# RMSNorm on one core: uneven tiles, a third tile loaded in 29 and 2 rows, and a first store that waits for the 29

## The chip, the core and the metric

The kernel runs on one core of one Trainium2 chip. The metric is the device time of one execution in microseconds (us), as the median of repeated runs. A separate execution, taken with the hardware profiler, gives the profile and the trace. In a profile PE is the matrix engine, DVE the vector engine, ACT the scalar engine, POOL the GpSimd engine and SP the engine that issues all DMAs of this kernel.

## The reference

```python
batch, seq, dim = 16, 1024, 512
x = np.random.randn(batch, seq, dim).astype(np.float32)      # 33.55 MB
gamma = np.ones(dim, dtype=np.float32)

def reference(x, gamma):
    eps = 1e-5
    rms = np.sqrt(np.mean(x ** 2, axis=-1, keepdims=True) + eps)
    return (x / rms * gamma).astype(np.float32)
```

There are 16384 rows of 512 numbers. Each is divided by the root of its mean square and multiplied by gamma. All of x is read once and all of the output is written once, 67.1 MB in total.

## The kernel before

**Tiles.** The 16384 rows are cut into 4 tiles of 4096 rows. In a tile each of the 128 partitions holds R = 32 consecutive rows of 2 KB, so that a partition's part of a tile is one stretch of 64 KB in memory. Below, "a row" means one row in each of the 128 partitions, which is 256 KB. The whole kernel loads 128 such rows and stores 128.

**Buffers.** Three buffers (`slot0` to `slot2`) of 32 rows hold tiles 0, 1 and 2; tile 3 goes into `slot0` again, after tile 0 has been stored from it (`slot_of = [0, 1, 2, 0]`). All work is done in place in these buffers.

**DMA order.** Every load (helper `load`, line 45) and every store (helper `store`, line 49) is issued by SP, in program order, on one queue. A DMA instruction that has to wait for something holds back all later ones on SP. The order is: tile 0 in 1, 15 and 16 rows (gamma's 2 KB after the first two), tile 1 in 16 and 16, tile 2 in 16 and 16; then two stores of 16 rows for tile 0; then two loads of 16 rows for tile 3 into the same buffer, each waiting until the store of those rows has landed; then one store of 32 rows for tile 1, one for tile 2, and two of 16 rows for tile 3. The function `transfers` places those after the first five loads.

**Compute.** The tiles are worked through in 8 groups of 16 rows, written out in the list `groups` as (tile, first row, rows, pieces, POOL's share). For a group, `square_sums` squares pieces of several rows on ACT (L95) into a scratch buffer and adds them up on DVE (L96); `inverse_rms` makes the factor of each row (L101 on ACT, L102 on DVE). Then POOL multiplies its share of rows by the factor and by gamma (L108, L109); ACT multiplies the other rows by the factor, row by row (L117), and DVE multiplies these by gamma (L121). The squares of the next group are interleaved with the scaling of this one.

**Scratch.** The squares go alternately into a PSUM buffer of 7 rows and an SBUF buffer of 5 rows. The two groups of tile 0 have pieces of 7 and 9 rows, and the piece of 9 uses the last rows of `slot2` as scratch, before tile 2 is loaded there:

```python
        if m == 9:
            sq = slots[2][:, 23:32, :]
```

So the load of rows 16 to 32 of tile 2 has to wait until DVE has added up the second such piece; the load of its rows 0 to 16 does not.

Of the kernel before, what the change touches and what calls it, by code (L numbers as in the profile page):

```python
# [8 lines left out]
@with_exitstack  # L9
def kernel(  # L10
    ctx: ExitStack,
    tc: tile.TileContext,
    x: bass.AP,
    gamma: bass.AP,
    out: bass.AP,
):
    nc = tc.nc
    P = nc.NUM_PARTITIONS
    eps = 1e-5
    fp32 = mybir.dt.float32  # L20
    AF = mybir.ActivationFunctionType
    OP = mybir.AluOpType

    xf = x.flatten_outer_dims()
    of = out.flatten_outer_dims()
    N, D = xf.shape
    R = 32
    assert N == 4 * P * R

    xv = xf.rearrange("(t p r) d -> t p r d", p=P, r=R)  # L30
    ov = of.rearrange("(t p r) d -> t p r d", p=P, r=R)

    ctx.enter_context(tc.manual_schedule())
    nc.scalar.addr_align(128, offset=0, max_nops=0)

    const = ctx.enter_context(tc.tile_pool(name="const", bufs=1))
    stats = ctx.enter_context(tc.tile_pool(name="stats", bufs=9))
    psum = ctx.enter_context(tc.tile_pool(name="psum", bufs=1, space=bass.MemoryType.PSUM))

    slots = [const.tile([P, R, D], fp32, name=f"slot{i}") for i in range(3)]  # L40

    before_scale = []

    def load(t, slot, r0, r1):
        dma = nc.sync.dma_start(out=slots[slot][:, r0:r1], in_=xv[t][:, r0:r1])  # L45
        before_scale.append((slot, r0, r1, dma))

    def store(t, slot, r0, r1):
        dma = nc.sync.dma_start(out=ov[t][:, r0:r1], in_=slots[slot][:, r0:r1])
        before_scale.append((slot, r0, r1, dma))  # L50

    gamma_row = const.tile([1, D], fp32)
    pieces = (0, D)

    load(0, 0, 0, 1)
    load(0, 0, 1, 16)
    for c0, c1 in zip(pieces, pieces[1:]):
        nc.sync.dma_start(out=gamma_row[:, c0:c1], in_=gamma.unsqueeze(0)[:, c0:c1])
    load(0, 0, 16, 32)
    load(1, 1, 0, 16)  # L60
    load(1, 1, 16, 32)

    ones_col = const.tile([1, P], fp32)
    nc.gpsimd.memset(ones_col, 1.0)  # L64
    gamma_psum = psum.tile([P, 1, D], fp32, name="gamma_psum")
    nc.tensor.matmul(gamma_psum[:, 0], ones_col, gamma_row, start=True, stop=True)  # L66
    gamma_b = const.tile([P, 1, D], fp32)

    eps_t = const.tile([P, 1], fp32)
    nc.gpsimd.memset(eps_t, eps)  # L70
    table = const.tile([P, 1], fp32)
    nc.scalar.activation(out=table, in_=eps_t, func=AF.Sqrt)  # L72

    groups = [
        (0, 0, 16, (7, 9), 6),
        (0, 16, 16, (7, 9), 7),
        (1, 0, 16, (7, 5, 4), 7),
        (1, 16, 16, (7, 5, 4), 7),  # L80
        (2, 0, 16, (7, 5, 4), 7),
        (2, 16, 16, (7, 5, 4), 7),
        (3, 0, 16, (7, 5, 4), 7),
        (3, 16, 16, (7, 5, 4), 3),
    ]
    slot_of = [0, 1, 2, 0]

    def square_sums(ss, t, g, r, m, k):
        if m == 9:
            sq = slots[2][:, 23:32, :]  # L90
        else:
            home, name, most = ((psum, "sq_psum", 7), (const, "sq_sbuf", 5))[k % 2]
            sq = home.tile([P, most, D], fp32, name=name)
        rows = slots[slot_of[t]][:, g + r : g + r + m, :]
        nc.scalar.activation(out=sq[:, :m], in_=rows, func=AF.Square)  # L95
        nc.vector.tensor_reduce(  # L96
            out=ss[:, r : r + m, 0], in_=sq[:, :m], axis=mybir.AxisListType.X, op=OP.add
        )

    def inverse_rms(ss, n):  # L100
        nc.scalar.activation(out=ss[:, :n, 0], in_=ss[:, :n, 0], func=AF.Sqrt, bias=eps_t, scale=1.0 / D)  # L101
        nc.vector.reciprocal(out=ss[:, :n, 0], in_=ss[:, :n, 0])  # L102
        return ss

    def scale_by_pool(rstd, t, g, n, share):
        part = slots[slot_of[t]][:, g + n - share : g + n, :]
        by_row = rstd[:, n - share : n].to_broadcast([P, share, D])
        nc.gpsimd.tensor_tensor(out=part, in0=part, in1=by_row, op=OP.mult)  # L108
        last = nc.gpsimd.tensor_tensor(  # L109
            out=part, in0=part, in1=gamma_b.to_broadcast([P, share, D]), op=OP.mult  # L110
        )
        before_scale.append((slot_of[t], g + n - share, g + n, last))

    def scale(rstd, t, g, r0, r1):
        x = slots[slot_of[t]]
        for r in range(r0, r1):
            nc.scalar.activation(out=x[:, g + r, :], in_=x[:, g + r, :], func=AF.Copy, scale=rstd[:, r])  # L117

    def times_gamma(t, g, r0, r1):
        part = slots[slot_of[t]][:, g + r0 : g + r1, :]  # L120
        scaled = nc.vector.tensor_tensor(  # L121
            out=part, in0=part, in1=gamma_psum.to_broadcast([P, r1 - r0, D]), op=OP.mult
        )
        for slot, b0, b1, earlier in before_scale:
            if slot == slot_of[t] and b0 < g + r1 and g + r0 < b1:
                tc.declare_no_dep(scaled.ins, earlier.ins, reason="ScalarE waited for it before it scaled these rows")

    def transfers(t, g):
        if (t, g) == (0, 0):
            load(2, 2, 0, 16)  # L130
            load(2, 2, 16, 32)
        elif (t, g) == (0, 16):
            store(0, 0, 0, 16)
            store(0, 0, 16, 32)
            load(3, 0, 0, 16)
            load(3, 0, 16, 32)
        elif (t, g) == (1, 16):
            store(1, 1, 0, 32)
        elif (t, g) == (2, 16):
            store(2, 2, 0, 32)  # L140
        elif (t, g) == (3, 0):
            store(3, 0, 0, 16)
        elif (t, g) == (3, 16):
            store(3, 0, 16, 32)

    def pieces_of(group):
        t, g, n, pieces, share = group
        ss = stats.tile([P, 16, 1], fp32, name="ss")
        r = 0
        todo = []  # L150
        for k, m in enumerate(pieces):
            todo.append((ss, t, g, r, m, k))
            r += m
        return ss, todo

    ss, todo = pieces_of(groups[0])
    for piece in todo:
        square_sums(*piece)
    rstd = inverse_rms(ss, groups[0][2])
    nc.scalar.copy(out=gamma_b[:, 0], in_=gamma_psum[:, 0])  # L160
    for k, group in enumerate(groups):
        t, g, n, pieces, share = group
        mine = n - share
        half = (mine + 1) // 2
        ahead = groups[k + 1 :][:1]
        ss, todo = pieces_of(ahead[0]) if ahead else (None, [])
        scale_by_pool(rstd, t, g, n, share)
        for piece in todo[:2]:
            square_sums(*piece)
        scale(rstd, t, g, 0, half)  # L170
        for piece in todo[2:]:
            square_sums(*piece)
        scale(rstd, t, g, half, mine)
        times_gamma(t, g, 0, mine)
        transfers(t, g)
        for nxt in ahead:
            rstd = inverse_rms(ss, nxt[2])
# [30 lines left out]
```

## Time and profile before

| what | value |
|---|---|
| median of 3 runs | 161.75 us (161.73 to 161.88) |
| profiled execution: its own time | 161.72 us |
| profiled execution: span from the first to the last instruction | 159.9 us |
| bytes moved by DMA | 67.12 MB, 420 GB/s over the span |
| DVE, ACT, POOL busy | 112.8, 109.1, 102.1 us |
| share of the 16 DMA engines' time in data packets | 98.1% |

The profile's times count from the start of the span. An issue row gives the time on SP and the median time from issue to landing, that is to the semaphore which says that the data is there. "DMA share" in a window is the time of the packets that begin in it, so it can exceed 1 in a short window.

### The profile page before, as it was taken

To read this page: it belongs to the slowest core of one execution; us is meant where nothing else is said; L and a number is where in the kernel's file an instruction comes from. 1 tells how busy PE (TensorE), PEld (TensorE's weight loads), DVE (VectorE), ACT (ScalarE), POOL (GpSimd) and SP (SyncE) were. 2 spreads that over 40 slices of the span, in tenths; PEclk is the share of its full clock that TensorE was granted. 3 is DMA by queue.
4 is the path that set the end of the run, shared out by engine and by line. 5 is a ranking of instruction groups with operands and counts; after the bars stand their busy time and mean duration, and the time that the engine had idled before them with its cause. 6 is when DMAs were issued, how large, how long until landed. Compare 5 with 4: busy or idle time off the path is not lost.

```text
span 159.9 us, 258 instructions
## 1 busy us (share of the span) xinstructions
PE 2.0 (1%) x2; PEld 0.5 (0%) x2; DVE 112.8 (71%) x38; ACT 109.1 (68%) x110; POOL 102.1 (64%) x22
## 2 busy tenths in 40 slices
PE   0005000000000000000000000000000000000000
PEld 0001000000000000000000000000000000000000
DVE  0000993797999999999999999999999702950000
ACT  3007906999998899899989989999994297000000
POOL 1000005994079999999999999999999997000000
DMA  5989999999999997999999999997997998999995
GB/s 191 492 369 468 451 393 434 484 393 418 484 410 393 483 426 311 483 393 402 508 402 393 492 426 393 524 475 311 524 459 328 524 426 361 393 459 459 393 426 229
DMA packets 2163, 67.12 MB, mean 420 GB/s; under 512 B 241, under 2 KB 241, under 8 KB 370
## 3 DMA queue, kind: packets, MB, share of 16 engines
q1 hardware_dynamic: 2162, 67.11, 98.1%
q14 instruction: 1, 0.01, 0.0%
HBM read 33.56 MB, written 33.55 MB: 420 GB/s over the span
## 4 chain that ended last, share of the span: by engine, by line
DVE 62%; ACT 18%; DMA 7%; ACTq 0%; SPq 0%; issue 0%
DVE ss L96 36%; DVE slot L121 26%; ACT slot L117 9%; DMA slot<-in_x_dram 7%; ACT slot L95 5%; ACT sq_psum L95 4%; DVE ss L102 1%; ACTq L203 0%; ACT gamma_b L160 0%; SPq L45 0%; ACT ss L101 0%; ACTq L95 0%
## 5 line engine op out<-in xcount | busy, mean ns | idle before, releaser
L108 POOL TENSOR_TENSOR slot<-slot,ss 128x3584 f32<-128x3584 f32 (+2 forms) x8 | 45.0, 5625 | 31.8 <-DVE ss L102 31.8
L96 DVE TENSOR_REDUCE ss<-sq_psum 128x7 f32<-128x3584 f32 (+1 forms) x14 | 44.5, 3176 | 19.5 <-ACT sq_psum L95 19.5
L109 POOL TENSOR_TENSOR slot<-slot,gamma_b 128x3584 f32<-128x3584 f32 (+2 forms) x8 | 56.9, 7112 | 0.6
L117 ACT ACTIVATE slot<-slot,ss 128x512 f32<-128x512 f32 x77 | 48.5, 707 | 4.9 <-DVE ss L102 4.9
L121 DVE TENSOR_TENSOR slot<-slot,gamma_psum 128x4608 f32<-128x4608 f32 (+2 forms) x8 | 42.3, 5282 | 9.3 <-ACT slot L117 9.3
L95 ACT ACTIVATE sq_psum<-slot 128x3584 f32<-128x3584 f32 (+1 forms) x14 | 36.5, 2604 | 11.4 <-DMA slot<-in_x_dram 10.4
L96 DVE TENSOR_REDUCE ss<-sq_sbuf 128x5 f32<-128x2560 f32 x6 | 16.8, 2806 | 0.0
L95 ACT ACTIVATE sq_sbuf<-slot 128x2560 f32<-128x2560 f32 x6 | 13.9, 2320 | 0.0
L96 DVE TENSOR_REDUCE ss<-slot 128x9 f32<-128x4608 f32 x2 | 9.9, 4953 | 0.1
L101 ACT ACTIVATE ss<-ss,eps_t 128x16 f32<-128x16 f32 x8 | 2.4, 306 | 8.4 <-DVE ss L96 8.4
L95 ACT ACTIVATE slot<-slot 128x4608 f32<-128x4608 f32 x2 | 8.1, 4028 | 0.0
L102 DVE RECIPROCAL ss<-ss 128x16 f32<-128x16 f32 x8 | 2.0, 249 | 0.4 <-ACT ss L101 0.4
L66 PE MATMUL gamma_psum<-gamma_row,ones_col 1*128 1x512 f32 x2 | 2.0, 1120 | 12.8 <-DMA gamma_row<-in_gamma_dram 12.8
L72 ACT ACT_TABLE_LOAD x1 | 1.3, 1283 | 1.1 <-PEq L192 1.1
L160 ACT COPY gamma_b<-gamma_psum 128x512 f32<-128x512 f32 x1 | 0.6, 566 | 0.0
L66 PEld LDWEIGHTS gamma_psum<-gamma_row,ones_col 1*128 1x128 f32 x2 | 0.5, 304 | 12.8 <-issue 12.8
L64 POOL MEMSET ones_col<- 1x128 f32 x1 | 0.2, 194 | 0.3 <-POOLq L192 0.3
L192 POOL MEMSET const-float32-0.0<- 128x1 f32 x1 | 0.1, 98 | 0.2 <-issue 0.2
L72 ACT ACTIVATE table<-eps_t 128x1 f32<-128x1 f32 x1 | 0.2, 203 | 0.0
L192 POOL MEMSET const-bfloat16-1.0<- 128x1 bf16 x1 | 0.1, 101 | 0.0
L192 POOL MEMSET const-uint8-127<- 128x1 uint8 x1 | 0.1, 101 | 0.0
L192 POOL MEMSET const-float32-1.0<- 128x1 f32 x1 | 0.1, 98 | 0.0
(1 smaller groups left out, 0.1 us busy)
## 6 DMA issues: line engine op xcount, KB each, us to landing
slot<-in_x_dram SPq DMA_DIRECT2D x7, 4096.0 KB, 27.1
out_dram<-slot SPq DMA_DIRECT2D x4, 4096.0 KB, 21.8
slot<-in_x_dram SPq DMA_DIRECT2D x1, 3840.0 KB, 11.8
slot<-in_x_dram SPq DMA_DIRECT2D x1, 256.0 KB, 3.1
out_dram<-slot SPq DMA_DIRECT2D x2, 29.2
gamma_row<-in_gamma_dram SPq DMA_DIRECT2D x1, 2.0 KB
```

Of the source, the lines that this page charges most:

```text
L66: nc.tensor.matmul(gamma_psum[:, 0], ones_col, gamma_row, start=True, stop=True)
L72: nc.scalar.activation(out=table, in_=eps_t, func=AF.Sqrt)
L95: nc.scalar.activation(out=sq[:, :m], in_=rows, func=AF.Square)
L96: nc.vector.tensor_reduce(out=ss[:, r : r + m, 0], in_=sq[:, :m], axis=mybir.AxisListType.X, op=OP.add)
L101: nc.scalar.activation(out=ss[:, :n, 0], in_=ss[:, :n, 0], func=AF.Sqrt, bias=eps_t, scale=1.0 / D)
L102: nc.vector.reciprocal(out=ss[:, :n, 0], in_=ss[:, :n, 0])
L108: nc.gpsimd.tensor_tensor(out=part, in0=part, in1=by_row, op=OP.mult)
L109: last = nc.gpsimd.tensor_tensor(out=part, in0=part, in1=gamma_b.to_broadcast([P, share, D]), op=OP.mult)
L117: nc.scalar.activation(out=x[:, g + r, :], in_=x[:, g + r, :], func=AF.Copy, scale=rstd[:, r])
L121: scaled = nc.vector.tensor_tensor(out=part, in0=part, in1=gamma_psum.to_broadcast([P, r1 - r0, D]), op=OP.mult)
L160: nc.scalar.copy(out=gamma_b[:, 0], in_=gamma_psum[:, 0])
L192: nc = _bacc.Bacc("TRN2", target_bir_lowering=False, num_devices=1)
```

## The change

The tiles become uneven: 33, 31, 31 and 33 rows per partition. The three buffers have 33, 31 and 31 rows. The second group of each tile has 17, 15, 15 and 17 rows, and its last piece of squares changes by one row. The scratch piece in `slot2` covers rows 21 to 31, of which a piece of 9 uses the first 9 and the new piece of 10 uses all.

Tile 2 is loaded as one DMA of 29 rows and one of 2 rows. The load of 29 rows covers scratch rows, so it waits for DVE, too. The first store (rows 0 to 16 of tile 0) gets an added wait: SP issues it only when the load of the 29 rows has landed.

```diff
-    R = 32
-    xv = xf.rearrange("(t p r) d -> t p r d", p=P, r=R)
-    ov = of.rearrange("(t p r) d -> t p r d", p=P, r=R)
+    rows_of = (33, 31, 31, 33)
+    def by_tile(flat):
+        views, start = [], 0
+        for rows in rows_of:
+            part = flat[start : start + P * rows]
+            views.append(part.rearrange("(p r) d -> p r d", p=P, r=rows))
+            start += P * rows
+        return views
...
-    def store(t, slot, r0, r1):
+    def store(t, slot, r0, r1, behind=None):
         dma = nc.sync.dma_start(out=ov[t][:, r0:r1], in_=slots[slot][:, r0:r1])
+        if behind is not None:
+            tc.add_manual_dep(
+                dma.ins,
+                behind.ins.name,
+                mybir.DependencyInfo(mybir.DependencyClass.Sync, mybir.DependencyReason.DATA),
+                reason="the store is issued when this load has landed",
+            )
...
-        (0, 16, 16, (7, 9), 7),
+        (0, 16, 17, (7, 10), 7),
         (1, 0, 16, (7, 5, 4), 7),
-        (1, 16, 16, (7, 5, 4), 7),
+        (1, 16, 15, (7, 5, 3), 7),
         (2, 0, 16, (7, 5, 4), 7),
-        (2, 16, 16, (7, 5, 4), 7),
+        (2, 16, 15, (7, 5, 3), 7),
         (3, 0, 16, (7, 5, 4), 7),
-        (3, 16, 16, (7, 5, 4), 3),
+        (3, 16, 17, (7, 5, 5), 3),
...
-        if m == 9:
-            sq = slots[2][:, 23:32, :]
+        if m >= 9:
+            sq = slots[2][:, 21:31, :]
...
         if (t, g) == (0, 0):
-            load(2, 2, 0, 16)
-            load(2, 2, 16, 32)
+            gate.append(load(2, 2, 0, 29))
+            load(2, 2, 29, 31)
         elif (t, g) == (0, 16):
-            store(0, 0, 0, 16)
-            store(0, 0, 16, 32)
+            store(0, 0, 0, 16, behind=gate[0])
+            store(0, 0, 16, 33)
             load(3, 0, 0, 16)
-            load(3, 0, 16, 32)
+            load(3, 0, 16, 33)
```

## The prediction

> **What bounds the kernel now.** I read the page's slices first, then the queues.
>
> ```profile
> span 159.9 us, 258 instructions
> ...
> DMA  5989999999999997999999999997997998999995
> GB/s 191 492 369 468 451 393 434 484 393 418 484 410 393 483 426 311 483 393 402 508 402 393 492 426 393 524 475 311 524 459 328 524 426 361 393 459 459 393 426 229
> ...
> q1 hardware_dynamic: 2162, 67.11, 98.1%
> ```
>
> The DMA engines work from the first slice to the last, and their packets fill 98.1% of the span. No compute engine passes 71%. So only DMA time that is idle or stretched can be won, 1.9% of 159.9, about 3 us, start and end included.
>
> Next, the DMA view in narrow windows, each around one issue on SP: bytes and time from issue to landing (loads issued at 2.02 and 38.01, stores at 44.71, 58.95, 86.93, 114.93 and 142.22).
>
> ```profile
> slot<-in_x_dram SPq DMA_DIRECT2D x1, 4096.0 KB, 20.7
> ...
> slot<-in_x_dram SPq DMA_DIRECT2D x1, 4096.0 KB, 24.2
> ...
> out_dram<-slot SPq DMA_DIRECT2D x1, 4096.0 KB, 27.2
> ...
> out_dram<-slot SPq DMA_DIRECT2D x1, 4096.0 KB, 23.0
> ...
> out_dram<-slot SPq DMA_DIRECT2D x1, 33.5
> ...
> out_dram<-slot SPq DMA_DIRECT2D x1, 24.9
> ...
> out_dram<-slot SPq DMA_DIRECT2D x1, 4096.0 KB, 16.9
> ```
>
> Issue plus time gives landings; with the other issues' rows and the longest load (3.40 + 48.4) they are: 16 rows at 13.0 us, 32 at 22.7, 48 at 32.4, 64 at 42.1, 80 at 51.8, 96 at 62.2; stores at 71.9 and 81.95; loads until 101.1; stores at 120.4, 139.8, 149.5 and 159.1. The step is 9.7 us per 16 rows (0.606 per row) nearly everywhere. 51.8 to 62.2 is 10.4: the changeover from loads to the first store costs 0.7 us more than any load step. The second such changeover (101.1 to 120.4 for 32 rows) shows nothing beyond 19.4.
>
> The trace's single packets say the same from nearer. A 32 KB packet takes 1.21 us on each of the 16 DMA engines. Before the first store, the last load packet takes 1.69 to 2.04 us, and on five engines the one before it 0.25 to 0.41 more than normal. On the engine that is last here, the last load packet takes 2.04 (0.83 over) and its first store packet begins at 61.88. Before the second changeover packets are stretched by 0.28 at most, and in the first 9 us by some tenths. Otherwise the packets follow each other without gaps.
>
> **What waits.** The views of DVE and SP around the scratch and around the first stores:
>
> ```profile
> 28.97 4.03 ACT L95 ACTIVATE slot<-slot 128x4608 f32<-128x4608 f32 x1
> ...
> 33.03 4.95 DVE L96 TENSOR_REDUCE ss<-slot 128x9 f32<-128x4608 f32 x1
> 38.01 0.33 SPq L45 DMA_DIRECT2D slot<-in_x_dram  x1
> ...
> 44.71 0.35 SPq L49 DMA_DIRECT2D out_dram<-slot  x1
> ```
>
> The second half of tile 2 is issued as soon as DVE's sum frees the scratch. The first store is issued at 44.71, long before the loads ahead of it are through.
>
> **The change, part by part.**
>
> *Same bytes, other cuts.* 128 rows in and 128 out, 15 large DMAs as before. Packets of 34, 58 and 62 KB stand in for 32 and 64 KB. Packet records: 1.213 us for 32 KB, 2.418 for 64 KB. The difference is 0.008 us per 64 KB. The load of 29 rows has 8 packets on each engine in place of 14.5: at most 0.06 us. I take 0.02. That a partition's stretch is now 66 or 62 KB instead of 64 could ease or hurt the start, where 14 engines had a packet stretched by 0.03 to 0.51 us; I bound it by 0.3 us to both sides and take nothing.
>
> *Tile 2 comes later into the queue.* Before, its first 16 rows were issued at 3.40, now all of it waits for the sum of the 10-row piece. ACT: 4.03 + 512 x (4.03 - 2.32)/2048 = 4.46 us (from the 4608 and 2560 rows), done at 33.43. DVE starts there instead of at 33.03 and takes 4.95 + 512 x (4.95 - 2.80)/2048 = 5.49, done at 38.95. Issue at 38.98. The first load of the kernel was issued at 0.74, and the first packets on the 16 engines began between 1.74 and 2.22: a lead of 1.0 to 1.48 us. So tile 2 is ready in the queue by 40.0 to 40.5. The 64 rows ahead of it (33 + 31, as 32 + 32 before) end on the engines between 41.10 and 41.65 by the packet records. That is a cover of at least 0.6 us, and the cost is nothing; if DVE slipped by more than that, each further us would cost one.
>
> *The first store moves from 44.71 to the landing of the 29 rows.* The late engine of before had the data of 80 rows by 51.36. After 93 rows (64 + 29) it is at 51.36 + 13 x 0.605 = 59.22. Landing follows data by 0.47 (51.83 against 51.36): 59.69. SP issues within 0.02 to 0.08 after a landing (the load at 71.90 follows the store landing at 71.88): 59.75. With the lead of 1.0 to 1.48, store packets begin at 60.75 to 61.23. The 2 rows keep this engine busy until 59.22 + 1.21 + 0.04 = 60.47 (0.04 for small packets: a 2 KB packet takes 84 ns where 76 would match the 32 KB rate). Idle: 0.28 to 0.76 us.
>
> The bar: before, this engine began to store at 61.88 with 96 rows loaded. With 95 rows the same progress is 61.88 - 0.61 = 61.27. If the stretch of the last load packets goes away once no store is queued behind them, the gain is 0.04 to 0.52 us. I take the middle, 0.28. The lead is from the only idle start in the trace, of a load that has to fetch from memory; a store's own lead is not shown. Bounds: a lead of 0.6 at the low end of what I allow gives a gain of 0.9, about the whole stretch of 0.83; a lead as long as issue to landing of the first 256 KB (3.1 us) less its 0.6 of data, 2.5, gives packets at 62.25, a loss of 1.0. I stand nearer the lead that packets show.
>
> A rule speaks against this wait. The Trainium skill, "DMA: Bandwidth & Descriptors", section "Rules for kernel authors", wants DMAs issued early so that the fixed setup cost overlaps, and at least 1 MiB each; the load of 2 rows is 0.5 MB. The same page's section "Anatomy of one DMA" gives the fixed part of one DMA as about 2.0 us, measured on another issue path. By it the store would start at 59.22 + 2.0 = 61.22, and the gain would be an estimated 0.05 us. The rows' own total (0.47 + 0.06 + 1.0 to 1.48) is 1.5 to 2.0.
>
> *Behind the wait on SP* stand store 0b and both loads of tile 3. Store 0b was issued at 58.95 when POOL had finished. POOL and DVE move by about 0.43 (ACT's longer piece), and DVE has one row more there: both are done near 59.4, before SP is free at 60.15. Store 0b has until the 16 rows of the first store are through, about 70.5. The first load of tile 3 follows the first store's landing (71.9 before, within a few tenths now), covered by 17 rows of store 0b, 10 us. If that cover were gone it would cost a lead, 1.0 to 1.5 us.
>
> *Compute.* The groups change by a row here and there; DVE, ACT and POOL keep their totals of rows. The delay of 0.43 and one more ACT row at the end (0.71) put the last store at about 143.4 instead of 142.22. The store before it holds the DMA engines until about 149, so even with a lead of 1.5 there are 4 us to spare. Nothing on the end.
>
> **Sum.** Span and own time: 159.9 and 161.72, 0.03 from the median of 161.75. So 161.75 - 0.28 = 161.47; with the 0.02 from longer packets, **161.45 us**.
>
> **Rivals.** A difference below 0.2%, 0.32 us, is about what a measurement of this kernel can't tell from none: faster means under 161.43, slower over 162.07.
>
> 1. *The wait costs little and the stretch goes* (0.56): 161.2 to 161.7, with 161.45 in the middle. Half of it lies under 161.43. For it: the stretch comes exactly where loads and a queued store meet.
> 2. *The whole stretch is won* (0.14): lead near 0.6, and the uneven stretches ease the start. 161.75 - 0.83 = 160.9, up to 161.2. For it: 0.83 us are there to win. Against it: no row shows such a lead.
> 3. *The idle gap takes the stretch's place, and more* (0.26): the stretch stays with any change from loads to stores, or is paid by the first store, and the lead comes on top. Store packets at 61.23 and then the old 0.83 less the 0.04 to 0.3 that fall into idle time: 61.8 to 62.0 against the bar of 61.27, 0.5 to 0.8 us slower, 162.25 to 162.5. For it: the stretch begins near 59.4, when store 0b was issued, and two stores will now be issued in exactly that stretch. Against it: the second changeover stretched packets by 0.28 at most. It decides from a total of more than 2.4 us between the end of the 29 rows and the first store packet (61.6).
> 4. *The scratch holds back tile 2* (0.04): DVE's sum ends over 0.6 us later than worked out. Each us beyond costs one; 162.1 to 163.
>
> **How the numbers follow.** Faster: half of 1 and all of 2, 0.28 + 0.14 = 0.42. Same: the other half of 1, 0.28. Slower: 0.26 + 0.04 = 0.30. The range takes in case 1, most of case 2 and the nearer part of case 3: 160.95 to 162.4.
>
> **What would show it.** In the profile after: tile 2's issue near 39.0 with no hole in the DMA slices at 40 to 44 us; the first store's issue near 59.75 and store 0b's near 60.15; the first store's landing before 71.3 (71.9 less the 0.61 of the row that no longer precedes it) if time is won, after 71.6 if it is lost; last load packets of normal length; no change in steps from there on. A landing of the 29 rows far from 59.7, packets stretched elsewhere, or a last store that waits for compute would make the prediction wrong.

## The result and the profile after

The changed kernel takes 163.36 us in the median (163.25 to 164.05, 6 runs) against 161.81 (161.68 to 162.11, 6 runs) for the kernel before: a ratio of 1.010, 95% interval 1.0088 to 1.0111. It is 1.55 us slower. The profiled execution took 163.26 us with a span of 161.5.

The page of the changed kernel, its slices and the share of the data queue:

```profile
span 161.5 us, 258 instructions
...
DMA  5989999999999789999999999899959996999995
GB/s 189 487 374 475 440 441 390 451 426 449 509 471 397 338 336 520 390 406 414 414 390 430 495 414 397 363 409 503 503 252 503 503 472 283 438 463 390 414 466 224
...
q1 hardware_dynamic: 2162, 67.11, 97.8%
```

The DMA engines are as full as before, 97.8% of a span that is 1.6 us longer. The rest of the span is 3.0 us before and 3.6 after, so about 0.5 of the 1.6 us is idle time, and about 1.1 went into packets that took longer for the same bytes. Which ones, the landings tell. Here is the DMA view of the changed kernel in narrow windows, around the issues at 39.00, 59.76, 60.23, 82.21, 87.84 and 143.09 (bytes, then time from issue to landing):

```profile
slot<-in_x_dram SPq DMA_DIRECT2D x1, 7424.0 KB, 20.7
...
out_dram<-slot SPq DMA_DIRECT2D x1, 4096.0 KB, 11.2
...
out_dram<-slot SPq DMA_DIRECT2D x1, 4352.0 KB, 22.0
...
slot<-in_x_dram SPq DMA_DIRECT2D x1, 4352.0 KB, 21.0
...
out_dram<-slot SPq DMA_DIRECT2D x1, 7936.0 KB, 34.2
...
out_dram<-slot SPq DMA_DIRECT2D x1, 4352.0 KB, 17.6
```

Before the change the last load was issued at 81.97, and the window around that issue reads:

```profile
slot<-in_x_dram SPq DMA_DIRECT2D x1, 4096.0 KB, 19.1
```

| landed | rows through, before / after | before | after | after minus before, same rows |
|---|---|---|---|---|
| first store | 112 / 111 | 71.9 | 70.9 | -0.35 |
| second store | 128 / 128 | 81.95 | 82.2 | +0.24 |
| last load | 160 / 161 | 101.1 | 103.2 | +1.55 |
| store of tile 1 | 192 / 192 | 120.5 | 122.0 | +1.55 |
| last store | 256 / 256 | 159.12 | 160.65 | +1.53 |

(Where the rows differ by one, 0.61 us is set off.) The wait does what it was costed at: the first store lands 0.35 us ahead of schedule. Then 0.6 us are lost before the second store has landed and 1.3 before the last load has, at the changeovers from stores to loads and from loads to stores. After that both kernels keep step.

The same in single packets, which the tables below use: for each of the 16 DMA engines, the time of its packets above the normal rate of 27 GB/s and the gaps between them, as a mean over the engines.

| changeover | before | after |
|---|---|---|
| 1: loads to stores, near 60 | 0.88 stretch | 0.54, of it 0.48 idle |
| 2: stores to loads, near 81 | 0.00 | 0.85 stretch |
| 3: loads to stores, near 100 | 0.13 | 1.07 stretch |
| sum | 1.01 | 2.46 |

The difference, 1.45 us, is nearly all of the 1.55. The added idle time is that of the first changeover, where it took the place of a larger stretch; the loss is the stretch at the second and third.

### The profile page after: what moved, and what is told of

Read it like the earlier page. It is cut to its first block, busy times and chain, and to the rows that moved or that the text cites. A ratio compares the mean times of both kernels' runs of the same rounds, so it can differ in the third digit from the quotient of the medians.

```text
span 161.5 us, 258 instructions
## 1 busy us (share of the span) xinstructions
PE 2.0 (1%) x2; PEld 0.5 (0%) x2; DVE 113.0 (70%) x38; ACT 109.0 (67%) x110; POOL 102.2 (63%) x22
## 3 DMA queue, kind: packets, MB, share of 16 engines
q1 hardware_dynamic: 2162, 67.11, 97.8%
## 4 chain that ended last, share of the span: by engine, by line
DVE 59%; ACT 21%; DMA 7%; ACTq 0%; SPq 0%; issue 0%
DVE ss L112 32%; DVE slot L137 26%; ACT slot L133 11%; DMA slot<-in_x_dram 7%; ACT slot L111 5%; ACT sq_psum L111 5%; DVE ss L118 1%; ACTq L221 0%; ACT gamma_b L178 0%; SPq L53 0%; ACT ss L117 0%; ACTq L111 0%
## 5 line engine op out<-in xcount | busy, mean ns | idle before, releaser
L112 DVE TENSOR_REDUCE ss<-sq_psum 128x7 f32<-128x3584 f32 (+3 forms) x14 | 43.9, 3137 | 19.6 <-ACT sq_psum L111 19.6
L137 DVE TENSOR_TENSOR slot<-slot,gamma_psum 128x4608 f32<-128x4608 f32 (+3 forms) x8 | 42.3, 5283 | 9.5 <-ACT slot L133 9.4
L111 ACT ACTIVATE sq_psum<-slot 128x3584 f32<-128x3584 f32 (+3 forms) x14 | 36.0, 2571 | 13.0 <-DMA slot<-in_x_dram 10.4
L112 DVE TENSOR_REDUCE ss<-slot 128x9 f32<-128x4608 f32 (+1 forms) x2 | 10.4, 5220 | 0.6 <-ACT slot L111 0.5
L111 ACT ACTIVATE slot<-slot 128x4608 f32<-128x4608 f32 (+1 forms) x2 | 8.5, 4242 | 0.0
L117 ACT ACTIVATE ss<-ss,eps_t 128x16 f32<-128x16 f32 (+2 forms) x8 | 2.5, 307 | 7.1 <-DVE ss L112 7.0
L118 DVE RECIPROCAL ss<-ss 128x16 f32<-128x16 f32 (+2 forms) x8 | 2.0, 249 | 0.4 <-ACT ss L117 0.4
```

Source lines behind the costliest of these rows:

```text
L112: nc.vector.tensor_reduce(out=ss[:, r : r + m, 0], in_=sq[:, :m], axis=mybir.AxisListType.X, op=OP.add)
L137: scaled = nc.vector.tensor_tensor(out=part, in0=part, in1=gamma_psum.to_broadcast([P, r1 - r0, D]), op=OP.mult)
```

## The experiments

Each run is of a kernel that computes the whole reference. "Toll" below is the extra time at a changeover, measured as in the last table, in the one profiled execution of each kernel; medians and ranges are over all executions.

### Which half of the change does it

**gate_even**: the wait without the uneven tiles. Tile 2 is loaded in 30 and 2 rows, which the wait needs; what that cut does by itself, uneven_no_gate shows below.

```diff
-            load(2, 2, 0, 16)
-            load(2, 2, 16, 32)
+            gate.append(load(2, 2, 0, 30))
+            load(2, 2, 30, 32)
...
-            store(0, 0, 0, 16)
+            store(0, 0, 0, 16, behind=gate[0])
```

> The wait alone: four tiles of 32 rows as before the change, tile 2 loaded in 30 and 2 rows, first store issued when the 30 have landed. Theory A (the stretched packets at the later two changeovers, 1.8 us in the changed kernel, come with the cut into 33, 31, 31 and 33 rows): the gain at the first changeover stays, the later two stay near 0.1 us, total 161.2 to 161.5 (faster by 0.3 to 0.5). Theory B (they come from the wait: it restarts all DMA engines at the same moment, and later changeovers meet in step): later changeovers stretch by 0.7 us and more each, 162.8 to 163.4.

Measured: 163.38 us (163.24 to 163.48, 4 runs) against 161.88, ratio 1.0089 (1.0074 to 1.0104). Tolls 0.46 (0.40 idle), 0.84, 1.16. Its windows around the issues at 60.24, 60.71, 82.14 and 86.85:

```profile
out_dram<-slot SPq DMA_DIRECT2D x1, 4096.0 KB, 11.2
...
out_dram<-slot SPq DMA_DIRECT2D x1, 4096.0 KB, 21.4
...
slot<-in_x_dram SPq DMA_DIRECT2D x1, 4096.0 KB, 20.6
...
out_dram<-slot SPq DMA_DIRECT2D x1, 35.2
```

Landings at 71.4, 82.1, 102.7 and 122.0: the last load is 1.6 us later than before the change, on tiles that are not uneven.

**uneven_plain**: the uneven tiles alone. From the changed kernel:

```diff
-            gate.append(load(2, 2, 0, 29))
-            load(2, 2, 29, 31)
+            load(2, 2, 0, 16)
+            load(2, 2, 16, 31)
...
-            store(0, 0, 0, 16, behind=gate[0])
+            store(0, 0, 0, 16)
```

> The uneven tiles alone: 33, 31, 31 and 33 rows, tile 2 loaded in 16 and 15 rows, no added wait. Theory A: the later changeovers stretch as in the changed kernel, total 162.5 to 164. Theory B: 161.5 to 162.0, as before the change.

Measured: 161.93 us (161.73 to 162.48) against 161.88, ratio 1.0007 (0.9997 to 1.0018). Tolls 0.88, 0.03, 0.08.

**uneven_no_gate**: the changed kernel without `behind=gate[0]`.

> The changed kernel without its added wait: uneven tiles, tile 2 in 29 and 2 rows, the first store issued as soon as its rows are ready, near 45 us. Theory A: first changeover stretched by about 0.8 again, later two by 1.8 together, 163.7 to 164.3. Theory B: first changeover stretched, later two not, 161.7 to 162.1.

Measured: 162.10 us (161.88 to 164.02, 10 runs), ratio 1.0023 (0.9998 to 1.0048). Tolls 1.13, 0.01, 0.08. Theory A has fallen: the cut of the tiles, and of tile 2 into 29 and 2 rows, costs nothing that this measurement resolves, and the loss is the wait's. One of the 10 executions took 164.02 us, 1.9 above the median. So a loss of this size can come without the wait, too; where it fell no trace shows.

**after_back**: the changed kernel with the tiles taken from the end of the memory.

```diff
-        views, start = [], 0
+        views, end = [], N
         for rows in rows_of:
-            part = flat[start : start + P * rows]
+            part = flat[end - P * rows : end]
...
-            start += P * rows
+            end -= P * rows
```

> The changed kernel with the tiles taken from the end of x and of the output towards the beginning: same instructions, sizes and order, other memory addresses. If the stretch at a changeover depends on which addresses the last transfer and the next one touch: the later two changeovers change by 0.3 us or more each, total outside 163.0 to 163.7. If on sizes and order alone (theories A in its plain form, and B): 163.3, within 0.2.

Measured: 163.36 us (163.04 to 164.03, 4 runs), ratio 1.0093 (1.0066 to 1.012). Tolls 0.62, 0.85, 1.04. Taking the tiles in the reverse order changed neither the time nor the later tolls.

Theory B named a cause as well, that the wait lets all engines start in step. The traces speak against that part. At the landing of the first load of tile 3 the engines of gate_even are 0.52 us apart (91.27 to 91.79), those of the kernel before 0.52 as well (90.82 to 91.34), and yet the next toll is 1.16 in the one and 0.13 in the other. So I looked for another state that the wait leaves behind.

### What the wait leaves behind

**gate_cover4**: gate_even with 28 and 4 rows, so that the store is in the queue before the loads end.

```diff
-            gate.append(load(2, 2, 0, 30))
-            load(2, 2, 30, 32)
+            gate.append(load(2, 2, 0, 28))
+            load(2, 2, 28, 32)
```

> The wait on even tiles with twice the cover: tile 2 in 28 and 4 rows, the first store issued when the 28 have landed. The last 4 rows keep the DMA engines busy for 2.4 us, longer than landing, issue and lead together (1.3 to 1.4 us after the landing of the 30 rows here), so they do not run dry. Theory I (running dry is what makes the later changeovers dear): the first changeover stretches by about 0.9 again, the later two by 0.15 or less, total 161.6 to 162.1. Theory W (the late issue itself does): later two stretch by 0.8 and 1.1 as in the run with 2 rows of cover, 163.2 to 163.8.

Measured: 163.21 us (163.04 to 163.37, 2 runs) against 161.74, ratio 1.0094 (1.0065 to 1.0123). Its windows around the store issued at 59.13, the load at 81.31 and the store at 86.94:

```profile
out_dram<-slot SPq DMA_DIRECT2D x1, 4096.0 KB, 12.1
...
slot<-in_x_dram SPq DMA_DIRECT2D x1, 4096.0 KB, 21.4
...
out_dram<-slot SPq DMA_DIRECT2D x1, 35.2
```

The first changeover is free: no gap, no stretched packet; store packets follow the loads between 60.5 and 61.05, with the store in the queue since about 60.0 (an estimate: issue at 59.13 and the lead of 0.84 to 1.00 of the changed kernel). But the tolls after it are 0.40 and 1.04 in the mean, where Theory W had 0.8 and 1.1. They are unequal over the engines, the last of which ends 1.98 us after the first. So Theory I was wrong: running dry is not needed. A first changeover that costs nothing at all also leaves the later two dear.

**gate_cover8**: the same with 24 and 8 rows.

> The wait on even tiles with a cover of 8 rows: tile 2 in 24 and 8 rows, the first store issued when the 24 have landed, so that it stands in the queue for some 3.5 us before the loads end (4 rows: about 1.1 us; before the change: 15 us). Theory Q (the toll of about 0.9 us falls on the first changeover for which the next transfer was queued well ahead, and only there it makes the later ones free): the first changeover stretches by 0.8 to 1.0 again, the later two by 0.15 or less, 161.6 to 162.1. Theory W (a wait on a landing before the first store is enough to make the later two dear, whatever its cover): first below 0.2, later two 0.4 to 1.2 each, 163.0 to 163.6.

Measured: 161.79 us (161.6 to 162.12, 10 runs) against 161.73, ratio 1.0005 (0.9997 to 1.0014). Tolls 0.99, 0.00, 0.20. Windows around the stores issued at 56.70 and 58.94, the load at 82.10 and the store at 86.96:

```profile
out_dram<-slot SPq DMA_DIRECT2D x1, 4096.0 KB, 15.5
...
out_dram<-slot SPq DMA_DIRECT2D x1, 4096.0 KB, 23.1
...
slot<-in_x_dram SPq DMA_DIRECT2D x1, 4096.0 KB, 19.4
...
out_dram<-slot SPq DMA_DIRECT2D x1, 33.9
```

The last load lands at 101.5, the store of tile 1 at 120.9, within 0.5 us of the kernel before, in the slowest of the 10 executions. With the wait still there, but the store in the queue from about 57.6, some 3 us ahead of the loads' end (60.5 to 61.05 where they are not stretched, as in gate_cover4), all is as before the change: a toll at the first changeover and two that are nearly free. With 0.4 to 1.1 us ahead there was no toll at the first and one at each of the later two. The size of the last load is not what decides: in uneven_no_gate it is 2 rows as well, the store is queued long before, and the later two are free.

**alt**: five changeovers. Before the change, but the second half of tile 2 is loaded behind the first store.

```diff
             load(2, 2, 0, 16)
-            load(2, 2, 16, 32)
...
             store(0, 0, 0, 16)
+            load(2, 2, 16, 32)
             store(0, 0, 16, 32)
```

> Before the change, but with the second half of tile 2 issued behind the first store: loads and stores alternate in blocks of 16 rows, five changeovers instead of three, no added wait. Theory E (one stretched changeover from loads to stores sets the DMA engines right for all later ones, until they run dry): about 0.9 once, at the first, and 0.15 or less at the others, 161.7 to 162.2. Theory C (each changeover of a given kind has its price, the second kind free only by chance): 162.5 or more.

Measured: 162.34 us (161.96 to 162.9, 7 runs) against 161.74, ratio 1.0036 (1.0017 to 1.0055). Tolls in order: 0.99, 0.00, 0.10, 0.00, 0.04: one toll, not three or five. They are those of the fastest execution, 161.96 us. The median is 0.14 us above Theory E's range, and what the slower executions paid no trace shows.

**alt_gate**: the same with `load(2, 2, 0, 14)`, `load(2, 2, 14, 16)` and the first store behind the 14 rows.

> The same alternation, with the first store waiting for the first 14 rows of tile 2, whose last 2 rows are the cover. Theory E: idle 0.4 to 0.6 at the first changeover, about 0.85 and 1.1 at the second and third, then 0.15 or less at the fourth and fifth, 163.1 to 163.6. Theory C: every later changeover costs 0.8 to 1.1, 164.8 to 165.6.

Measured: 163.84 us (163.67 to 164.0, 2 runs), ratio 1.0133 (1.0104 to 1.0163). Tolls in order: 0.46 (0.40 idle), 0.85, 1.09, 0.00, 0.04. This is Theory E's picture: after the changeover with the wait the next two pay, and once a changeover from loads to stores has been stretched, later ones of both kinds are free. Theory C had 0.8 to 1.1 at the last two as well, and has fallen. The total is 0.2 us above the range; some load packets between 42.5 and 46 were stretched by 0.17 us in the mean.

**idle_stores**: before the change, but the second store waits for the first one's landing.

```diff
-            store(0, 0, 0, 16)
-            store(0, 0, 16, 32)
+            gate.append(store(0, 0, 0, 16))
+            store(0, 0, 16, 32, behind=gate[0])
```

> Before the change, with one wait elsewhere: the second store is issued only when the first store has landed, so that the DMA engines run dry for about 1.1 us between two stores, after an ordinary first changeover. Theory I/E (running dry is what counts, wherever it happens): beside the 1.1 us the later two changeovers stretch by 0.85 and 1.1, 164.5 to 165.2. Theory F (what counts is that the first changeover was made across an idle gap): later changeovers stay below 0.15 each, 162.7 to 163.2.

Measured: 165.40 us (165.24 to 165.56, 2 runs) against 161.74, ratio 1.023 (1.020 to 1.026), 0.2 us above the range. First changeover 1.02; then a gap of 1.7 us between the stores, where 1.1 was expected; then 0.80 and 1.17 at the later two. The slices of its page show the gap and what follows it:

```profile
DMA  5999899998998989968969899999899979899994
GB/s 186 480 425 448 384 472 424 408 488 384 456 440 384 504 264 488 408 256 384 512 296 472 384 472 368 408 416 512 368 400 512 464 304 512 384 416 432 432 432 208
```

A wait between two stores, away from any changeover, makes the later two dear although the first one had been stretched. So the wait's place at the first changeover is not special, and Theory F has fallen. In this run the queue runs dry and a store is issued late, on a landing; it does not tell the two apart. In gate_cover4 the late issue was enough.

### Can all tolls be avoided?

**gate_all4**: each changeover made like the first one of gate_cover4 (`hold` is the added dependency of `store` as a function of its own; `load` gets it, too).

```diff
-            store(0, 0, 16, 32)
-            load(3, 0, 0, 16)
-            load(3, 0, 16, 32)
+            gate.append(store(0, 0, 16, 28))
+            store(0, 0, 28, 32)
+            load(3, 0, 0, 16, behind=gate[1])
+            gate.append(load(3, 0, 16, 28))
+            load(3, 0, 28, 32)
...
-            store(1, 1, 0, 32)
+            store(1, 1, 0, 32, behind=gate[2])
```

> Even tiles, and all three changeovers made as the first one in the run with 4 rows of cover: the loads of tile 3 issued when the first 28 of the 32 stored rows of tile 0 have landed, the store of tile 1 when the first 28 rows of tile 3 have. Theory Q: no changeover has the next transfer queued well ahead, so none pays: stretch below 0.2 at each, 160.8 to 161.2 (faster than both kernels by 0.6 to 1.0). Theory T (the toll is only put off and is paid at some changeover, or as idle time): 161.8 to 163.4.

Measured: 162.02 us (161.68 to 163.54, 12 runs) against 161.73, ratio 1.0035 (1.0014 to 1.0056). Tolls 0.01, 0.51 (1.4 on the worst engine), 0.19 (0.16 idle), in an execution of 162.56 us. The time is within Theory T's range.

**gate_434** and **gate_424**: the same with 3 and 2 rows of cover at the second changeover.

```diff
-            gate.append(store(0, 0, 16, 28))
-            store(0, 0, 28, 32)
+            gate.append(store(0, 0, 16, 29))
+            store(0, 0, 29, 32)
```

> As the run with 4 rows of cover at all three changeovers, but 3 rows at the second (from stores to loads), where the 4 rows still let packets stretch by 0.5 us in the mean and by 1.4 on the worst engine, with the loads ready for about 1 us before the stores ended. Theory Q (what is queued ahead decides): with about 0.4 us in the queue the second changeover stretches by 0.2 or less, the other two by 0.1: 160.8 to 161.4, faster than before by 0.2% or more. Theory T (the toll falls due anyway): the third changeover or idle time takes it over, 161.7 to 162.6.

> The same with 2 rows of cover at the second changeover. Theory Q: no stretch there, but 0.2 to 0.5 us of idle time, 161.0 to 161.6. Theory T: 161.7 to 162.6.

Measured: 162.61 us (162.48 to 162.98, 6 runs) and 162.67 us (162.65 to 162.83, 5 runs) against 161.70; ratios 1.0057 (1.0042 to 1.0072) and 1.0058 (1.0045 to 1.0071). Tolls of gate_434: 0.01, 0.99 (0.16 idle), 0.00; of gate_424: 0.01, 1.38 (0.78 idle), 0.00. Theory Q fails at the second changeover: from stores to loads the toll came with 4, 3 and 2 rows of cover alike. From loads to stores a late queue did avoid it, twice in each of these two runs. Theory T had the time nearly right (up to 162.6) and the place wrong, for the toll stayed at the second changeover. In each of the three kernels 0.7 to 1.4 us is left in all, idle time included, where the kernel before has 1.01. In gate_434 the data end at 159.03, against 158.77 before the change; the rest of its loss lies behind the data, with four instructions more in the program: own time minus span is 2.1 us instead of 1.8. No version beat the kernel before.

## Why the prediction was wrong, point by point

- **The gate itself: right.** Store issue at 59.76 (foretold 59.75), tile 2's issue at 39.00 (38.98) with no hole after it, second store at 60.23 (60.15), last store's issue at 143.09 (143.4). The landing of the 29 rows came at 59.69, as worked out. The SP view of the changed kernel, issues merged in pairs:

```profile
39.00 0.80 SPq L53 DMA_DIRECT2D slot<-in_x_dram  x2
59.76 0.82 SPq L58 DMA_DIRECT2D out_dram<-slot  x2
```

- **The lead: a little long.** Store packets began at 60.60 to 60.76, a lead of 0.84 to 1.00 us instead of 1.0 to 1.48. The gain at the first changeover was 0.35 by landings, within the 0.04 to 0.52 of the sum, and the first store landed before 71.3, the mark set for "time is won". The estimate from a figure of the Trainium skill ("DMA: Bandwidth & Descriptors", section "Anatomy of one DMA"), a fixed 2.0 us taken as the time from the end of the 29 rows to the store's data, was too long: the 29 rows ended by 59.23, so it was 1.4 to 1.5.
- **The step that failed: "no change in steps from there on".** The stretch at the first changeover went away, as case 1 said, but the sum stopped there and took the prices of the second and third (nothing, and 0.28 at most) as fixed properties of these places. They are not. They are low where the first one has been paid. In every profiled kernel the first store queued 3 us or more ahead of its changeover paid about 1 us there, and after it changeovers of both kinds cost 0.2 at most, until a store was issued so late that it stood in the queue for about 1 us or less before its turn. After such a late store the next changeover to loads cost 0.4 to 0.85 us of stretch, and the first one to a store queued well ahead 1.04 to 1.17. The missing term is 0.85 + 1.07 - 0.13 = 1.8 us; with the gain of 0.35 it makes 1.45, the measured loss but for 0.1. The profile of before had the fact in view, tolls of 0.88, 0.00 and 0.13 at three changeovers, and I read the two low ones as the natural price and the high one as an accident of a queued store.
- **The rivals.** Case 3 had the right sign and the wrong place: it let the stretch come at the first changeover, on top of the lead, for 0.5 to 0.8 us. That changeover was 0.35 us cheaper than before. Its argument that the stretch began when store 0b was issued falls with idle_stores, where 0b is issued at 72.22 and the first changeover still costs 1.02. Its doubt, that the second changeover from loads to stores had stretched packets by only 0.28, was the same misreading. Case 4, the scratch, did not happen. In case 2 a lead of 0.6 could have won 0.8 and not 0.9, as the 2 rows keep the engine busy until 60.47.
- **Uneven tiles: right.** They were put at a gain of 0.02 us, and uneven_plain shows no difference that can be measured.
- **Not settled.** What in the DMA engines holds this state, and why a stretched changeover from loads to stores makes the following ones free, no trace here shows. Nor does one show whether running dry undoes it without a late issue. How long a store has to be queued ahead for the toll to fall on its changeover lies between 1 us (gate_cover4) and 3 us (gate_cover8); it was not narrowed further.

## What to carry to other kernels

In a kernel that keeps the DMA engines full, cost every later change of direction anew when one is altered: a price of nothing may have been bought by an earlier one. Be wary of a store that is issued just in time, behind the last load or behind another store. With the later transfers queued well ahead, it cost 1.4 to 2.0 us at the changeovers after it, while a store queued 3 us or more ahead paid one toll of about 1 us and little more. Holding back the later transfers as well did not help: no such kernel beat the one before. Test such an edit alone, and read the landings beyond it, not only those at its place.

## What the runs showed of the hardware

- A change of direction can stretch packets by 0.8 to 1.2 us in the mean of the 16 DMA engines (0.4 and 0.5 in gate_cover4 and gate_all4), or not at all (0.00 at two of the five changeovers in alt). Which of the two depends on the history of the queue: alt and alt_gate have the same order of loads and stores, and their second changeover cost 0.00 and 0.85.
- With the queue about to run empty a store's first packets came 0.84 to 1.00 us after its issue on SP began; the landing of the 29 rows lagged their data by 0.46.
- Stretches of 62 or 66 KB per partition instead of 64 KB, and the reverse order of the tiles in memory, changed neither the packet rate (1.21 us for 32 KB) nor, by more than 0.1 us, the tolls.
